# Moving 16 more tokens from the dense expert matmuls to the gathered rows, spreading the rows over the stages, and splitting pieces of u two ahead

## The chip, the cores and the metric

The kernel runs on one core of one Trainium2 chip. The metric is the device time of one execution in microseconds (us); less is better. Engines are named as in the profile: PE (TensorE matmul), PEld (TensorE weight load), DVE (VectorE), ACT (ScalarE), POOL (GpSimd) and SP (SyncE, which only issues DMAs here).

## The reference, cut to what matters

One layer over 512 tokens of width 2048. The change lies in its last part, a retrieval over 16384 experts of one neuron each: every token picks 16 experts in each of 8 heads (128 in all), and with the rows `u` and `v` of those experts

```
act = gelu(einsum('thkd,td->thk', u[ib], tb))
out = einsum('thk,thkd->td', g * act, v[ib])
```

Ahead of it stand an input projection, a state-space group, an attention group and an output projection; after it a norm.

## The kernel before, in words

Numbers are fp32. Each weight piece of 512 KB is loaded by SP (`w_raw`), copied by ACT to a rounded `w_hi` (L80) and completed by DVE with `w_lo = w_raw - w_hi` (L81, in `wload`); three matmuls (hi·hi, hi·lo, lo·hi) then make one product. There are 5 buffers for `w_raw` and 4 each for `w_hi` and `w_lo`.

The 512 tokens are treated in two ways. The first TD = 368 go through **dense** matmuls with all 16384 experts: `up` (L815, matmuls L823 to L825) multiplies 128 blocks of `u` with the tokens, `gate` (L897, L899) multiplies the result `A` by a matrix `G` that is zero where an expert was not picked, `down` (L927 to L929) multiplies by `v`. A group is 8 blocks; there are 16 groups, and a group has 384 matmuls in `up` and 384 in `down`, each with TD columns. The last 144 tokens are **gathered** (`gather`): POOL fetches, by an indirect DMA, for 128 tokens at a time one picked row of `u` or `v` each (L752, a tile of 128x2048 that the text calls a row tile), and DVE either dots it with the token (L757) or adds it, scaled, to the token's sum (L769). 128 tokens need 128 row tiles of `u` and 128 of `v`. The remaining X = 16 tokens are stacked so that one tile serves all of them with 128 / X = 8 picks each, which takes 16 tiles of `u` and 16 of `v`. So there are 288 row tiles.

The order in time: the trunk; the token routing's scores; a **routing stage**, in which `up` runs on PE for blocks of the first 10 groups while DVE and ACT do the routing (`topk`, then `gates`, which build `G` 4 tokens at a time: DVE L716 and L719, 4 small matmuls L729); `A` of these groups is parked in HBM (`Ad`). Then a **middle stage** with `up` and `down` of the last 6 groups, and a **late stage** in which POOL loads the parked `A` (L962) and only `down` runs.

`tick` sets the pace of the gather in program order: after each block of `up`, and twice per 512 columns of `down`, it adds a share of the row tiles that are left, divided by the ticks that are expected. A row tile's use on DVE stands two tiles behind its fetch (LAG = 2); the four buffers are `sx` tiles with the tag S:

```
self.owed += share * self.left / max(self.todo - 2, 1)
while self.owed >= 1 and self.left:
    self.owed -= 1
    self.left -= 1
    next(self.ga, None)
```

PE's order is that of the code from the routing stage's `up` on. The other engines' order is made by a scheduler when the program is built, and each engine's queue is in order on the chip.

Of the kernel before, what the change touches and what calls it, by code (L numbers as in the profile page):

```python
# [19 lines left out]
P = 128  # L20
# [3 lines left out]
KC = 16  # L24
# [5 lines left out]
NE = 16384  # L30
DT = 3
DN = DT * P
X = 16
XS = P // X
TD = DN - X
GB = 8
# [2 lines left out]
NTG = -(-TD // TG)  # L39
NEG = -3.0e38  # L40
LATE = 9
G_FIRST = 0.3
LAG = 2
SIDE0 = -8.0
SIDE = 0.65
# [13 lines left out]
class K:  # L59
# [724 lines left out]
    def peer_init(self):  # L784
        self.NG = P // GB
        self.turn_ = 0
        self.Gd = self.dp.tile([P, NTG, P, TG], F32, name="Gd")
        self.idxx = self.cp.tile([P, X], U32, name="idxx")
        self.gx = self.cp.tile([P, X], F32, name="gx")
        self.Ad = {}  # L790
        self.idx3 = self.cp.tile([P, P], U32, name="idx3")
        self.g3 = self.cp.tile([P, P], F32, name="g3")
        self.ga = None
        self.left = 2 * (P + X)
        self.todo = LATE * GB * G_FIRST + (self.NG - LATE) * GB + (self.NG - 1) * GB
        self.owed = 0.0

    def tick(self, share=1.0):
# [13 lines left out]
        tag = ("mm", "at", "mm", "tp")[self.turn_]  # L812
        return self.pp.tile([P, TD], F32, name=tag, tag=tag, bufs=4 if tag == "mm" else 2)

    def up(self, hi, engines, side=None):  # L815

        nc = self.nc
        Th, Tl = self.T2
        A = self.sx.tile([P, HB, TD], F32, name="A", tag="A", bufs=2)
        for i in range(HB):  # L820
            ps = self.bank() if side is None else self.pp.tile([P, TD], F32, name="mm", tag="mm", bufs=4)
            for kc, wh, wl in self.wpieces(self.io["uT"][hi * HB + i], KC, (8, P), engines):
                nc.tensor.matmul(ps, wh, Th[:, kc, :TD], start=(kc == 0), stop=False)  # L823
                nc.tensor.matmul(ps, wh, Tl[:, kc, :TD], start=False, stop=False)  # L824
                nc.tensor.matmul(ps, wl, Th[:, kc, :TD], start=False, stop=(kc == KC - 1))  # L825
                if side and kc % 4 == 3:
                    side()
            nc.scalar.activation(A[:, i, :], ps, AF.Gelu)
            self.tick(G_FIRST if side else 1.0)
        return A  # L830

    def peer_prologue(self, tk, top):

        nc = self.nc
        self.peer_init()

        def main():
            ready = None
            for t in (DT,) + tuple(reversed(range(DT))) + (None,):
                if t is not None:  # L840
                    res = {}
                    for d in self.topk(t, tk, top[0][t], top[1][t], res):
                        yield d, None
                    if t == DT:
                        nc.vector.tensor_copy(self.idx3, res["eu"])
                        nc.vector.tensor_copy(self.g3, res["g"])
                        self.ga = self.gather()
                        continue
                    if t == DT - 1:
                        for i in range(XS):  # L850
                            ps_, js = slice(i * X, (i + 1) * X), slice(i * X, (i + 1) * X)
                            nc.sync.dma_start(self.idxx[ps_, :], res["eu"][P - X:, js])
                            nc.sync.dma_start(self.gx[ps_, :], res["g"][P - X:, js])
                    steps = self.gates(t, tk, res)
                    for d in steps:
                        if d[0] is None:
                            break
                        yield d
                if ready:
                    yield from ready  # L860
                ready = steps

        m, state, later = main(), {"due": SIDE0, "on": True}, []

        def side():
            for w in later[:]:
                w[0] -= 1
                if w[0] <= 0:
                    later.remove(w)
                    w[1]()  # L870
            state["due"] += SIDE
            while state["due"] > 0:
                d = next(m, None)
                if d is None:
                    state["on"] = bool(later)
                    return
                state["due"] -= d[0]
                if d[1]:
                    later.append([12 if d[1].__name__ == "turn" else 3, d[1]])

        hi = 0
        with self.tc.manual_schedule(engines={nc.tensor.engine}):
            while state["on"] or hi % 2:
                A = self.up(hi, (nc.vector,), side)
                self.Ad[hi] = self.dp.tile([P, HB, TD], F32, name=f"Ad{hi}")
                nc.scalar.dma_start(self.Ad[hi], A)
                hi += 1
        return hi // 2
# [54 lines left out]
    def peer(self, es, first):  # L943
# [11 lines left out]
        for gi in list(range(first, self.NG)) + list(range(first)):  # L955
            As = []
            for hi in (2 * gi, 2 * gi + 1):
                if gi >= first:
                    A = self.up(hi, (nc.vector,))
                else:  # L960
                    A = self.sx.tile([P, HB, TD], F32, name="A", tag="A", bufs=2)
                    nc.gpsimd.dma_start(A, self.Ad[hi])  # L962
                self.gate(hi, A, fu)
                As.append(A)
            if before:
                self.down(*before)
            before = gi, self.split(As, fu)
            if gi == self.NG - 1:
                x1 = self.t2.tile([P, DT, D], F32, name="x1e", tag="T2h", bufs=1)
# [106 lines left out]
```

## Time and profile before

| what | value |
|---|---|
| median of three runs | 3438.3 us (3426.32 to 3446.59) |
| profiled execution | 3429.34 us, span 3426.5 us |
| PE busy | 3278.7 us, 96% |
| DVE busy | 2313.2 us, 68% |
| DMA | 770.10 MB, mean 225 GB/s |

The span is the time from the first to the last instruction; it is 2.84 us less than the execution's own time. The profiled execution lies 9 us under the median. A busy share is a mean over stages that differ much; it says nothing about which engine a stage waits for.

### The profile page before, as it was taken

What the parts mean: (1) busy time and instruction counts of PE and PEld (TensorE: products, weight loads), DVE (VectorE), ACT (ScalarE), POOL (GpSimd) and SP (SyncE); (2) the same over time, 40 slices, a digit from 0 to 9 for tenths busy, and PEclk for the clock granted to TensorE, in tenths of its full rate; (3) what the DMA queues carried; (4) which work ended last, traced back from release to release, by engine and by line L of the source; (5) the groups of instructions that cost most, each with busy time, mean ns of one, the idle gap of its engine ahead of it and who ended that gap; (6) DMA issues with size and microseconds to landing.
All of it is one profiled execution on the core that took longest, in us unless ns stands there. A gap on an engine that the chain in (4) does not pass through costs nothing.

```text
span 3426.5 us, 46085 instructions
## 1 busy us (share of the span) xinstructions
PE 3278.7 (96%) x18217; PEld 3032.9 (89%) x18217; DVE 2313.2 (68%) x3287; ACT 1195.4 (35%) x1956; POOL 866.7 (25%) x539
## 2 busy tenths in 40 slices
PE   6999999999899989999999999999999999989997
PEld 4777866678799989999999999999999999889987
DVE  6475345552435896466665888888878888788885
ACT  3342233332322323463666323323322322222222
POOL 2000000001111251012000443343445444544440
PEclk9999999999899999999999999999999999999999
DMA  3333322124322356466667998898998989899983
GB/s 134 98 102 99 111 74 68 63 95 138 121 90 87 105 197 224 161 227 223 220 229 254 342 362 328 335 353 325 357 371 324 352 324 344 311 340 320 342 321 118
DMA packets 207770, 770.10 MB, mean 225 GB/s; under 512 B 19441, under 2 KB 27633, under 8 KB 166449
## 3 DMA queue, kind: packets, MB, share of 16 engines
q1 hardware_dynamic: 146464, 375.06, 31.9%
q0 software_dynamic: 51408, 344.35, 26.5%
q10 hardware_dynamic: 9680, 47.75, 3.6%
q8 instruction: 142, 2.33, 0.3%
q14 instruction: 76, 0.61, 0.1%
HBM read 718.18 MB, written 48.89 MB: 224 GB/s over the span
## 4 chain that ended last, share of the span: by engine, by line
PE 69%; DMA 11%; DVE 9%; issue 6%; POOL 4%; ACT 1%; DVEq 0%; POOLq 0%; SPq 0%; ACTq 0%
PE mm L825 7%; PE mm L823 7%; PE mm L824 7%; DMA row<-in_v_dram,idx 5%; PE mm L116 3%; PE mm L118 3%; PE mm L117 3%; PE mm L102 3%; PE mm L104 3%; PE mm L103 3%; DVE w_lo L81 2%; DMA A<-Ad 2%; PE mm L927 2%; PE mm L928 2%; PE mm L929 2%
## 5 line engine op out<-in xcount | busy, mean ns | idle before, releaser
L80 ACT ACTIVATE w_hi<-w_raw 128x1024 fp32r<-128x1024 f32 x666 | 704.1, 1060 | 1667.6 <-PE mm L928 553.8
L81 DVE TENSOR_TENSOR w_lo<-w_raw,w_hi 128x1024 fp32r<-128x1024 f32 x648 | 811.7, 1263 | 610.8 <-ACT w_hi L80 599.6
L825 PE MATMUL mm<-T2h,w_lo 128*128 128x368 f32 x1664 | 549.6, 330 | 23.2 <-DVE w_lo L81 23.2
L823 PE MATMUL mm<-T2h,w_hi 128*128 128x368 f32 x1664 | 558.8, 336 | 0.5 <-ACT w_hi L80 0.5
L824 PE MATMUL mm<-T2l,w_hi 128*128 128x368 f32 x1664 | 547.3, 329 | 0.0
L752 POOL DMA_INDIRECT row<-in_u_dram,idx x128 | 197.5, 1543 | 788.2 <-DVE row L757 761.0
L769 DVE SCALAR_TENSOR_TENSOR x2g<-row,act,x2g 128x2048 f32<-128x2048 f32 x128 | 321.8, 2514 | 102.3 <-DMA row<-in_v_dram,idx 95.6
L928 PE MATMUL mm<-Wl,w_hi 128*128 128x368 f32 x1024 | 343.3, 335 | 0.0
L927 PE MATMUL mm<-Wh,w_hi 128*128 128x368 f32 x1024 | 343.0, 335 | 0.0
L929 PE MATMUL mm<-Wh,w_lo 128*128 128x368 f32 x1024 | 342.0, 334 | 0.0
L825 PEld LDWEIGHTS mm<-T2h,w_lo 128*128 128x128 f32 x1664 | 313.9, 189 | 29.3 <-DVE w_lo L81 29.3
L757 DVE SCALAR_TENSOR_TENSOR row<-row,h2n 128x2048 f32<-128x2048 f32 x128 | 323.3, 2543 | 0.0
L823 PEld LDWEIGHTS mm<-T2h,w_hi 128*128 128x128 f32 x1664 | 314.5, 189 | 1.0 <-ACT w_hi L80 0.9
L824 PEld LDWEIGHTS mm<-T2l,w_hi 128*128 128x128 f32 x1664 | 314.5, 189 | 0.0
L752 POOL DMA_INDIRECT row<-in_v_dram,idx x128 | 221.4, 1729 | 260.1 <-DVE x2g L769 227.3
L929 PE MATMUL at<-Wh,w_lo 128*128 128x368 f32 x512 | 175.3, 342 | 54.2 <-DVE w_lo L81 54.2
L116 PE MATMUL mm<-w_hi,T_hi 128*128 128x512 f32 x512 | 205.3, 401 | 0.0
L118 PE MATMUL mm<-w_hi,T_lo 128*128 128x512 f32 x512 | 203.3, 397 | 0.0
L117 PE MATMUL mm<-w_lo,T_hi 128*128 128x512 f32 x512 | 201.5, 394 | 0.0
L927 PEld LDWEIGHTS mm<-Wh,w_hi 128*128 128x128 f32 x1024 | 196.6, 192 | 0.0
L929 PEld LDWEIGHTS mm<-Wh,w_lo 128*128 128x128 f32 x1024 | 195.8, 191 | 0.0
L928 PEld LDWEIGHTS mm<-Wl,w_hi 128*128 128x128 f32 x1024 | 195.7, 191 | 0.0
(303 smaller groups left out, 6288.6 us busy)
## 6 DMA issues: line engine op xcount, KB each, us to landing
w_raw<-in_uT_dram SPq DMA_DIRECT2D x256, 512.0 KB
w_raw<-in_v_dram SPq DMA_DIRECT2D x256, 512.0 KB
w_raw<-in_wT_dram SPq DMA_DIRECT2D x58, 512.0 KB
Gd<-gb ACTq DMA_DIRECT2D x24, 1024.0 KB
G<-Gd POOLq DMA_DIRECT2D x32, 768.0 KB, 6.2
w_raw<-in_wN_dram SPq DMA_DIRECT2D x32, 512.0 KB
w_raw<-in_wo_dram SPq DMA_DIRECT2D x32, 512.0 KB
w_raw<-in_wq_dram SPq DMA_DIRECT2D x32, 512.0 KB
```

What stands on the lines that cost most here:

```text
L80: nc.scalar.activation(hi, raw, AF.Copy)
L81: sub = eng.tensor_sub(lo, raw, hi.bitcast(F32))
L116: nc.tensor.matmul(ps[t], Th[:, kc, s], wh, start=(kc == 0), stop=False)
L752: nc.gpsimd.indirect_dma_start(out=row, out_offset=None, in_=src, in_offset=bass.IndirectOffsetOnAxis(ap=idx[:, j:j + 1], axis=0))
L757: nc.vector.scalar_tensor_tensor(row, row, 1.0, h, op0=OP.mult, op1=OP.mult, accum_out=act[:, j:j + 1])
L769: nc.vector.scalar_tensor_tensor(acc, row, act[:, j:j + 1], acc, op0=OP.mult, op1=OP.add)
L823: nc.tensor.matmul(ps, wh, Th[:, kc, :TD], start=(kc == 0), stop=False)
L824: nc.tensor.matmul(ps, wh, Tl[:, kc, :TD], start=False, stop=False)
L825: nc.tensor.matmul(ps, wl, Th[:, kc, :TD], start=False, stop=(kc == KC - 1))
L927: nc.tensor.matmul(ps[j], vh, wh, start=f, stop=False)
L928: nc.tensor.matmul(ps[j], vh, wl, start=False, stop=False)
L929: nc.tensor.matmul(ps[j], vl, wh, start=False, stop=l)
```

## The change: what it does

X goes from 16 to 32. TD falls from 368 to 352, so all 12288 dense matmuls have 16 columns less. `NTG`, the number of 32-token pieces of the dense tokens, falls from 12 (the last one half full) to 11, so `gates` has 88 steps instead of 96, and the multiplication by `G` on POOL is one instruction instead of two. The stacked tokens take 32 + 32 row tiles instead of 16 + 16: 320 in all.

The pace: in the routing stage a block's tick counts 0.9 instead of 0.3, and in the late stage 0.9 instead of 1. `todo` follows. `upieces` replaces `wpieces` in `up`: in the routing stage it emits load and split of a piece of `u` two pieces before its matmuls, elsewhere just before them, as it was.

```diff
-X = 16
+X = 32
-G_FIRST = 0.3
+G_FIRST = 0.9
+G_LAST = 0.9
-        self.todo = LATE * GB * G_FIRST + (self.NG - LATE) * GB + (self.NG - 1) * GB
+        self.todo = LATE * GB * (G_FIRST + G_LAST) - GB * G_LAST + (self.NG - LATE) * GB * 2
-    def up(self, hi, engines, side=None):
+    def up(self, side=None):
-            for kc, wh, wl in self.wpieces(self.io["uT"][hi * HB + i], KC, (8, P), engines):
+            for kc, wh, wl in self.upieces(2 if side else 0):
+    def upieces(self, ahead):
+        for i in range(2):
+            while len(self.pre) <= ahead and self.npre < 2 * P:
+                b, k0 = self.npre // 2, 8 * (self.npre % 2)
+                self.pre.append(self.wload(self.io["uT"][b][:, k0:k0 + 8, :], [P, 8, P], self.nc.vector))
+                self.npre += 1
+            hi, lo = self.pre.pop(0)
+            for k in range(8):
+                yield 8 * i + k, hi[:, k, :], lo[:, k, :]
-                self.down(*before)
+                self.down(*before, 1.0 if gi >= first else G_LAST)
```

How it moves instructions, at three places.

POOL at the end of the routing stage, up to the first load of `G` (`tk_sel` belongs to `topk`, `row` is a row tile). Before:

```order
L752 DMA row<-in_u_dram,idx_8153 128x2048 x9
L673 TENSOR_TENSOR tk_sel<-tk_sel,tk_code 128x400 x11
L752 DMA row<-in_u_dram,idx_8153 128x2048
L673 TENSOR_TENSOR tk_sel<-tk_sel,tk_code 128x400
L752 DMA row<-in_u_dram,idx_8153 128x2048
L673 TENSOR_TENSOR tk_sel<-tk_sel,tk_code 128x400 x4
L752 DMA row<-in_u_dram,idx_8153 128x2048 x14
L894 DMA G<-Gd 128x12x128
```

The same place in the change:

```order
L753 DMA row<-in_u_dram,idx_8153 128x2048 x26
L674 TENSOR_TENSOR tk_sel<-tk_sel,tk_code 128x400
L753 DMA row<-in_u_dram,idx_8153 128x2048
L674 TENSOR_TENSOR tk_sel<-tk_sel,tk_code 128x400 x11
L753 DMA row<-in_u_dram,idx_8153 128x2048 x8
L674 TENSOR_TENSOR tk_sel<-tk_sel,tk_code 128x400 x4
L753 DMA row<-in_u_dram,idx_8153 128x2048 x37
L906 DMA G<-Gd 128x11x128
```

Counted over the whole queue, 32 row tiles stand ahead of the first load of `G` before and 84 in the change; between it and the first load of a parked `A` 133 and 134; from there on 123 and 102.

DVE in the routing stage, where one token tile's `topk` has ended and the next tile's routing steps have not come. Before:

```order
L666 CAST tk_pf<-tk_pu 128x128
L81 TENSOR_TENSOR w_lo<-w_raw,w_hi 128x1024 x4
L757 SCALAR_TENSOR_TENSOR row,act<-row,h2n 128x2048
L81 TENSOR_TENSOR w_lo<-w_raw,w_hi 128x1024 x6
L757 SCALAR_TENSOR_TENSOR row,act<-row,h2n 128x2048
L81 TENSOR_TENSOR w_lo<-w_raw,w_hi 128x1024 x4
```

In the change:

```order
L667 CAST tk_pf<-tk_pu 128x128
L82 TENSOR_TENSOR w_lo<-w_raw,w_hi 128x1024
L758 SCALAR_TENSOR_TENSOR row,act<-row,h2n 128x2048
L82 TENSOR_TENSOR w_lo<-w_raw,w_hi 128x1024 x2
L758 SCALAR_TENSOR_TENSOR row,act<-row,h2n 128x2048 x2
L82 TENSOR_TENSOR w_lo<-w_raw,w_hi 128x1024 x2
L758 SCALAR_TENSOR_TENSOR row,act<-row,h2n 128x2048
L82 TENSOR_TENSOR w_lo<-w_raw,w_hi 128x1024
L758 SCALAR_TENSOR_TENSOR row,act<-row,h2n 128x2048
L82 TENSOR_TENSOR w_lo<-w_raw,w_hi 128x1024
```

About every piece of `u` now has a dot of a row tile beside it. Counted per 10 pieces (`w_lo`) on DVE's queue, the routing stage has 1 to 3 uses of row tiles before, and 2 to 8 (mostly 6 to 8) in the change; the middle stage 7 or 8 in both; the late stage 7 or 8 before, and 6 or 7 in the change.

POOL in the late stage, one group of `down` (two loads of a parked `A`, two multiplications by `G`). Before:

```order
L962 DMA A<-Ad_10704 128x1472
L752 DMA row<-in_v_dram,idx_8153 128x2048
L897 TENSOR_TENSOR A<-A,G 128x4x352
L899 TENSOR_TENSOR A<-A,G 128x4x16
L752 DMA row<-in_v_dram,idx_8153 128x2048 x3
L894 DMA G<-Gd 128x12x128
L752 DMA row<-in_v_dram,idx_8153 128x2048 x8
L962 DMA A<-Ad_11117 128x1472
L752 DMA row<-in_v_dram,idx_8153 128x2048
L897 TENSOR_TENSOR A<-A,G 128x4x352
L899 TENSOR_TENSOR A<-A,G 128x4x16
L894 DMA G<-Gd 128x12x128
```

In the change:

```order
L974 DMA A<-Ad_10070 128x1408
L753 DMA row<-in_v_dram,idx_8153 128x2048
L909 TENSOR_TENSOR A<-A,G 128x1408
L753 DMA row<-in_v_dram,idx_8153 128x2048 x2
L906 DMA G<-Gd 128x11x128
L753 DMA row<-in_v_dram,idx_8153 128x2048 x7
L974 DMA A<-Ad_10418 128x1408
L753 DMA row<-in_v_dram,idx_8153 128x2048
L909 TENSOR_TENSOR A<-A,G 128x1408
L906 DMA G<-Gd 128x11x128
```

The shape of the group stays; it has about two row tiles less and one multiplication by `G` where there were two instructions.

## Rows read from the trace of the kernel before

**Rows 1.** The page: busy time of each engine, and the bytes moved in 40 equal slices of the span.

```profile
span 3426.5 us, 46085 instructions
...
PE 3278.7 (96%) x18217; PEld 3032.9 (89%) x18217; DVE 2313.2 (68%) x3287; ACT 1195.4 (35%) x1956; POOL 866.7 (25%) x539
...
GB/s 134 98 102 99 111 74 68 63 95 138 121 90 87 105 197 224 161 227 223 220 229 254 342 362 328 335 353 325 357 371 324 352 324 344 311 340 320 342 321 118
```

**Rows 2.** Busy time by stage: the stretch (us from the span's start), its length, busy time and count of instructions of each engine, granted clock of TensorE, busy share of the DMA engines, GB/s. The stages are the trunk with the scores, the routing stage, the middle stage, the late stage, the last `down`.

```profile
0.00:1127.00 1127.00, 1079.05 (x5063) 851.74 (x5063) 539.74 (x1165) 369.83 (x627) 83.01 (x60) 0.99 0.31 98
1127.00:1889.00 762.00, 738.31 (x4635) 731.65 (x4635) 519.43 (x1044) 380.83 (x834) 127.58 (x97) 0.99 0.58 206
1889.00:2595.00 706.00, 705.39 (x4210) 705.08 (x4209) 591.84 (x509) 220.55 (x249) 310.96 (x170) 1.00 0.92 348
2595.00:3338.00 743.00, 687.88 (x3922) 680.66 (x3921) 615.53 (x516) 205.00 (x214) 342.97 (x212) 0.96 0.89 330
3338.00:3426.50 88.50, 68.04 (x395) 63.74 (x394) 46.71 (x57) 19.17 (x34) 2.13 (x2) 0.92 0.34 127
```

**Rows 3.** The same view for single stretches of 100 us: one of the trunk, in which all matmuls have 512 columns; one early in the routing stage; two at the end of the middle stage.

```profile
800.00:900.00 100.00, 100.00 (x430) 80.43 (x429) 28.54 (x25) 23.24 (x33) 12.07 (x8) 1.00 0.30 95
1200.00:1300.00 100.00, 84.59 (x463) 81.08 (x462) 93.96 (x277) 28.75 (x35) 50.42 (x38) 0.95 0.56 195
...
2400.00:2500.00 100.00, 100.00 (x599) 100.00 (x598) 86.19 (x69) 31.04 (x34) 43.02 (x23) 1.00 0.95 359
2500.00:2600.00 100.00, 99.39 (x594) 99.08 (x593) 83.18 (x60) 31.20 (x34) 46.27 (x26) 1.00 0.97 363
```

**Rows 4.** Who waited for whom, PE alone: us in total, times, longest. First the routing stage, then the middle stage, then the late stage.

```profile
PE mm L825 <- DVE w_lo L81: 23.2, 19, 3.5
...
PE at L929 <- DVE w_lo L81: 0.6, 1, 0.6
...
PE at L929 <- DVE w_lo L81: 52.9, 21, 6.7
```

**Rows 5.** The same view for the late stage: DVE, then POOL.

```profile
DVE x2g L769 <- DMA row<-in_v_dram,idx: 95.6, 25, 6.4
...
POOL A L897 <- DMA A<-Ad: 125.9, 19, 10.5
```

**Rows 6.** Instructions of POOL in order of time, in the late stage, for one group: start, duration, instruction, and in brackets its idle time before it and what ended that.

```profile
3028.61 0.57 POOL L962 DMA_DIRECT2D A<-Ad  x1 [1.46 <-DVE Wl L909]
3030.84 0.96 POOL L752 DMA_INDIRECT row<-in_v_dram,idx  x1 [1.66 <-DVE x2g L769]
3037.85 4.95 POOL L897 TENSOR_TENSOR A<-A,G 128x1408 f32<-128x1408 f32 x1 [6.05 <-DMA A<-Ad]
3042.74 2.38 POOL L899 TENSOR_TENSOR A<-A,G 128x64 f32<-128x64 f32 x1
...
3046.53 0.57 POOL L962 DMA_DIRECT2D A<-Ad  x1
3047.41 1.96 POOL L752 DMA_INDIRECT row<-in_v_dram,idx  x1 [0.30 <-issue]
3057.75 3.23 POOL L897 TENSOR_TENSOR A<-A,G 128x1408 f32<-128x1408 f32 x1 [8.38 <-DMA A<-Ad]
...
3061.42 2.87 POOL L752 DMA_INDIRECT row<-in_v_dram,idx  x1 [0.16 <-issue]
```

**Rows 7.** Instructions of DVE in order of time, the same group.

```profile
3060.93 2.47 DVE L769 SCALAR_TENSOR_TENSOR x2g<-row,act,x2g 128x2048 f32<-128x2048 f32 x1 [6.14 <-DMA row<-in_v_dram,idx]
3063.33 2.35 DVE L81 TENSOR_TENSOR w_lo<-w_raw,w_hi 128x1024 fp32r<-128x1024 f32 x2
```

**Rows 8.** The routing stage, groups of instructions on DVE, then the small matmuls of `gates` on PE: shapes, count, busy us and mean ns of one, idle time before them and what ended it.

```profile
L81 DVE TENSOR_TENSOR w_lo<-w_raw,w_hi 128x1024 fp32r<-128x1024 f32 x160 | 199.3, 1254 | 146.4 <-ACT w_hi L80 146.3
L757 DVE SCALAR_TENSOR_TENSOR row<-row,h2n 128x2048 f32<-128x2048 f32 x30 | 70.6, 2354 | 0.0
L719 DVE TENSOR_TENSOR ga_A<-iota,ga_tr 128x512 f32<-128x512 f32 x96 | 66.9, 697 | 87.7 <-PE at L729 46.5 <-PE tp L729 41.1
L716 DVE TENSOR_TENSOR ga_B<-iota,ga_tr 128x512 f32<-128x512 f32 x96 | 65.7, 684 | 0.1
...
1652.52 1.05 PE L729 MATMUL tp<-ga_A,ga_B 128*128 128x128 f32 x8
1653.32 0.41 PE L823 MATMUL mm<-T2h,w_hi 128*128 128x368 f32 x1
```

**Rows 9.** DMA issues: count, KB each, median us to landing; and the second of the two multiplications by `G` in the late stage (count, busy us, mean ns).

```profile
G<-Gd POOLq DMA_DIRECT2D x32, 768.0 KB, 6.2
...
A<-Ad POOLq DMA_DIRECT2D x20, 736.0 KB, 9.7
...
L899 POOL TENSOR_TENSOR A<-A,G 128x64 f32<-128x64 f32 x20 | 25.7, 1284 | 0.0
```

More of the change, by code (lines that the diff above doesn't have):

```diff
@@ L879, in side @@
                     later.append([12 if d[1].__name__ == "turn" else 3, d[1]])
-        hi = 0
+        hi, self.pre, self.npre = 0, [], 0
         with self.tc.manual_schedule(engines={nc.tensor.engine}):
             while state["on"] or hi % 2:
-                A = self.up(hi, (nc.vector,), side)
+                A = self.up(side)
                 self.Ad[hi] = self.dp.tile([P, HB, TD], F32, name=f"Ad{hi}")
@@ L958, in peer @@
                 if gi >= first:
-                    A = self.up(hi, (nc.vector,))
+                    A = self.up()
                 else:
```

## The prediction

> **What bounds the kernel now.** I read the page first: PE is busy 96% of the span, DVE 68%, and the bytes moved rise from about 100 GB/s in the trunk to 310 to 371 in the second half [rows 1]. So a mean says little, and the next view is busy time by stage. The reader is to see four regimes in it [rows 2]. The trunk is untouched by the change. In the routing stage (762 us) PE is busy 738 us at 206 GB/s. In the middle stage (706 us) PE never rests and the DMA engines are busy 0.92 at 348 GB/s: here PE's matmuls alone set the time. In the late stage (743 us) PE is busy only 688 us, its granted clock is 0.96, and fewer bytes move, 330 GB/s. The waits say why. In the routing stage PE waits 23.2 us for `w_lo`, in the middle stage 0.6 us, in the late stage 52.9 us [rows 4]. Who holds `w_lo` up late? DVE waits 95.6 us for row tiles, and POOL, which issues them, stands 125.9 us waiting for parked `A` [rows 5]. In order of time it is one chain: POOL issues the load of `A` at 3028.61, waits, multiplies until 3045, issues the next load, waits 8.38 us, multiplies, and from 3030.84 to 3061.42 it has issued a single row tile, at 3047.41 [rows 6]. DVE runs out of row tiles, waits 6.14 us at 3060.93, and only then makes the next two `w_lo` [rows 7].
>
> How much does the late stage lose? In the middle stage, with PE always busy, 4210 matmuls take 706 us, 167.7 ns each [rows 2]. The late stage's 3922 would take 657.7 us at that pace; it takes 743, so 85 us are lost.
>
> **The matmuls' width.** A stretch in which all matmuls have 512 columns runs 430 in 100 us, 232.6 ns each [rows 3], against 167.7 ns at 368. That is 64.9 ns for 144 columns, 0.451 ns a column, so 16 columns are 7.2 ns. At 352 I take 160.5 ns. Where PE sets the time, 12288 matmuls give 88 us. The Trainium skill (TensorE: Matmul & The Clock Gate, Back-to-back issue gap) gives N/2.4 + 2.5 ns for a matmul at full clock; that is 155.8 ns at 368, where the trace has 167.7, and it would make the saving 6.67 ns and 82 us instead of 88. The measurement decides.
>
> **Routing stage.** 80 blocks of 48 matmuls save 3840 x 7.2 ns = 27.6 us. `gates` has 8 steps of 4 small matmuls less; 8 of these take 0.80 us until the next matmul starts [rows 8], so 32 are 3.2 us. Against that stand 52 more row tiles on DVE at 2354 ns (and about 0.08 us each to read the sum out, an estimate), 126 us, less 8 x (697 + 684) ns = 11 us of `gates` [rows 8]. DVE's 519 us become 634 of about 750, 85%; the middle stage has 592 of 706, 84%, and PE does not wait there [rows 2]. On the mean it fits. It doesn't fit everywhere: around 1200 to 1300 DVE is at 94% and PE falls to 84.6% [rows 3]; in this `topk` stretch the order has 4 row tiles more, 9.4 us. Where `gates` is dense, 10 pieces of `u` have some 28 instructions of it and 6.5 row tiles on DVE: 12 + 15.8 + 19.3 = 47 us, against 10 x 24 x 160.5 ns = 38.5 us of matmuls and 56 small ones at 0.1 us, 44 us in all. That is 3 us over for 10 pieces at worst, for some 35 of 160 pieces; with the idle ends between I take 10 us. Two pieces ahead (7.7 us of matmuls) can take back at most the 23.2 us that PE waits now [rows 4]; the added row tiles eat that cushion, and I take 0 for it. Sum: -27.6 - 3.2 + 9.4 + 10 = **-11 us**. Bounds: -54 (nothing added shows, the whole wait goes) and +120 (below).
>
> **Middle stage.** PE would need 4210 x 160.5 ns = 675.7 us, 30 us less. Row tiles are 134 against 133. The bytes stay: 348 GB/s x 706 us = 245.7 MB, plus one row tile (128 x 2048 x 4 bytes = 1.05 MB), less 12 loads of `G` smaller by a twelfth of 768 KB [rows 9], 245.9 MB. At PE's new pace that is 364 GB/s. No stretch shown holds that: two full-PE stretches run at 359 and 363 GB/s with the DMA engines 0.95 and 0.97 busy [rows 3]. Between the stage's mean of 348 and these I take 355: 693 us, **-13 us** (bounds 0 and -30).
>
> **Late stage.** PE's floor is 3922 x 160.5 ns = 629.5 us. The bytes are 330 x 743 = 245.2 MB less 21 row tiles (22.0), less 20 loads each of smaller `G` and `A` (1.3 and 0.7): 221.2 MB. At the rate of before, 330 GB/s, this takes 670 us; at the middle stage's 348, 636. What sets the rate is the chain, not the engines, which are only 0.89 busy [rows 2]. The chain is shorter by the second multiplication, 1.28 us for each `A` [rows 9], and DVE asks for a row tile every 629.5 / 102 = 6.2 us instead of 657.7 / 123 = 5.3 us, so the 30 us of [rows 6] starve it of five tiles instead of six. That favours the low end of the gain, and I take 335 GB/s: 660 us, **-83 us** (bounds -28, if the lost 85 us stay whole, and -113, if they vanish).
>
> **Last `down`.** 395 x 7.2 ns: **-3 us**. The pace's end fits better, too: 7 row tiles stand behind the last `A` instead of 13, which is in the late stage's sum.
>
> The stacked tokens' smaller edits (4 loads of `hx` instead of 8, routing indices in 4 loads instead of 8, on queues that do not hold PE) I cost at nothing; they hide under PE's matmuls. If they delayed DVE they would show in the routing stage, where the bound of +120 holds them.
>
> Sum: -11 - 13 - 83 - 3 = -110 us. Made against the profiled execution's 3429.3 us this is **3319 us**; that execution lies 9 us under the median, so a median of many runs would be some 9 us higher, well inside the range. About 0.5% (17 us) is what a measurement of this kernel can tell from no change; the runs of before spread over 20 us.
>
> **The rivals.**
>
> *The bytes flow as fast as asked for, up to a ceiling (20%).* If the late stage's chain is broken by the lower demand, PE or the DMA ceiling is left. With 361 GB/s, the mean of the two stretches of [rows 3], the middle stage takes 681 us (-25) and the late stage PE's 629.5 (-113): -11 - 25 - 113 - 3 = -152, **3277 us**. For it speaks that PE is full at 0.97 DMA share; against it that the late stage is not held by bandwidth. The Trainium skill (DMA: Bandwidth & Descriptors, Specifications) puts a core's share of HBM at about 358 GB/s; the trace's 363 is just over it, and with 358 the middle stage would be 687 us and the sum 3283.
>
> *The chain in the late stage stays as it is (15%).* The waits for parked `A`, 9.7 us from issue to landing [rows 9], and the order around them are unchanged. Then the 85 us stay: 629.5 + 85.3 = 715 us (-28), and if the middle stage can't exceed 348 GB/s it saves nothing. -11 + 0 - 28 - 3 = -42: **3387 us**.
>
> *Slower: DVE's queue sets the routing stage (6%).* DVE stands idle there some 248 us: 146.4 for `w_hi`, which waits for PE to free buffers, 87.7 for PE's small matmuls [rows 8], and a rest. If these waits are dictated by order and not by slack, the added work lies on top: 634 + 248 = 882 us instead of 762, +120 instead of -11, and **3450 us**, slower by 0.6%. It decides from the point where the stage takes 861 us, 99 more than before, which is what the other three stages give. Against it: both waits are waits for PE, so a later DVE finds them shorter. The remaining 4% are mixtures that end within 0.5%.
>
> **How the numbers follow.** Forecast 55%, the flowing bytes 20%, the unchanged chain 15%, slower 6%, near no change 4%. The first three end over 0.5% faster, so 0.90 faster, 0.04 same, 0.06 slower. The range takes the first three with some room: 3255 (below the ceiling case by the 23.2 us of the routing stage's waits) to 3395; the slow case lies outside.
>
> **What the profile would show.** Right: 100 us of the middle stage hold over 610 matmuls, with PE's wait near zero; the late stage is about 660 us long with 335 GB/s or more, PE's wait for `w_lo` there is roughly half of 53 us, DVE's wait for row tiles well under 96 us, and the granted clock is above 0.96. The routing stage moves about 280 GB/s with DVE near 85%, and is some 750 us long, PE's wait there no smaller than 23 us. Wrong: a routing stage longer than 800 us; PE waiting in the middle stage for `w_lo` whose cause is a DMA of `w_raw`, which would mean the rate of 348 was already the ceiling; or a late stage whose waits for `A` and row tiles add up as before.

## The result, and the profile after

The changed kernel takes 3319.9 us (median of four runs, 3313.6 to 3324.5) against 3437.7 us (3426.3 to 3446.6) for the kernel before, measured beside it: a ratio of 0.966 (95% interval 0.963 to 0.969). The forecast was 3319. The total is right, its terms are not: what the forecast gave to the routing stage has the wrong sign, and two others, for the middle and the late stage, were too small by about as much together.

The profiled execution took 3313.6 us. First its page, busy time of each engine.

```profile
span 3311.9 us, 45983 instructions
...
PE 3171.9 (96%) x18153; PEld 2926.7 (88%) x18153; DVE 2372.4 (72%) x3315; ACT 1175.1 (35%) x1908; POOL 882.6 (27%) x535
```

Then the changed kernel's routing, middle and late stage, in the columns of [rows 2].

```profile
1125.00:1904.00 779.00, 722.45 (x4590) 712.42 (x4589) 638.87 (x1141) 365.35 (x793) 231.16 (x155) 0.97 0.74 275
1904.00:2581.50 677.50, 676.91 (x4227) 676.62 (x4227) 583.91 (x445) 220.19 (x249) 282.71 (x155) 1.00 0.95 356
2581.50:3221.00 639.50, 622.07 (x3843) 618.60 (x3843) 560.99 (x502) 199.08 (x210) 285.18 (x165) 0.99 0.94 349
```

In the routing stage PE is now idle 56.5 us (779.0 - 722.45) where it was idle 24 [rows 2], and its granted clock has gone from 0.99 to 0.97. The middle stage is full of matmuls as before, only narrower: 677.5 us / 4227 = 160.3 ns each. In the late stage PE is idle 17 us where it was idle 55. In the routing stage the bytes have gone from 206 to 275 GB/s.

To compare kernels, all stages below are cut at the same events: the first matmul of the first group of `u` (start of the routing stage), that of the eleventh group (start of the middle stage), the first matmul of the sixth `down` (start of the late stage) and of the sixteenth, and the end of the span. By these marks, in us, from one profiled execution each:

| stage | before | after | difference | forecast |
|---|---|---|---|---|
| routing | 764.8 | 779.2 | +14.4 | -11 |
| middle | 708.6 | 677.3 | -31.3 | -13 |
| late | 729.6 | 639.2 | -90.4 | -83 |
| last `down` | 99.0 | 91.0 | -8.0 | -3 |
| span | 3426.5 | 3311.9 | -114.6 | -110 |

One stretch of 100 us of the middle stage answers to [rows 3], and then PE's waits to [rows 4]: three lines of the routing stage, one of the late stage.

```profile
2400.00:2500.00 100.00, 100.00 (x627) 100.00 (x626) 87.86 (x65) 32.11 (x35) 38.69 (x23) 1.00 0.91 341
```

```profile
PE mm L826 <- DVE w_lo L82: 33.3, 19, 6.4
PE tp L730 <- ACT ga_A L723: 19.1, 5, 8.6
PE at L730 <- ACT ga_A L723: 3.3, 3, 1.4
...
PE at L941 <- DVE w_lo L82: 15.5, 10, 4.0
```

The waits for `ga_A` (L730 are the small matmuls of `gates`) stand in no row of before: 22.4 us that are new. In the late stage PE's wait for `w_lo` fell from 52.9 to 15.5 us. The rows that answer to [rows 5], DVE and POOL in the late stage, say why:

```profile
DVE accx L770 <- DMA row<-in_v_dram,idxx: 18.2, 5, 6.9
DVE row L758 <- DMA row<-in_u_dram,idxx: 15.4, 6, 5.7
DVE x2g L770 <- DMA row<-in_v_dram,idx: 9.5, 6, 5.3
...
POOL A L909 <- DMA A<-Ad: 95.9, 19, 9.3
```

DVE's waits for row tiles fell from 106.3 us (the 95.6 of [rows 5] and 10.7 in two smaller lines) to 43.1 (these three), POOL's wait for parked `A` only from 125.9 to 95.9.

**Where the routing stage lost its time.** ACT's queue shows it. Its wait for the writes of `Gd` before the change:

```profile
ACT gb L731 <- DMA Gd<-gb: 56.0, 17, 6.7
```

and after it:

```profile
ACT gb L732 <- DMA Gd<-gb: 96.0, 18, 10.2
```

In `gates` the lines are these, unchanged but for their numbers (the scaling of `ga_A`, L723, stands ahead of `mm` in each step):

```
gb = [up.tile([P, 64, TG], F32, name="gb", tag="gb", bufs=2) for _ in range(2)]
...
        for i in range(2):
            nc.scalar.activation(gb[i][:, :, k4:k4 + 4], ...)
        if k4 + 4 == TG:
            for i in range(2):
                nc.scalar.dma_start(self.Gd[...], gb[i])
```

A piece is 32 tokens and fills two tiles; the tag has two buffers, and both belong to the same piece. So there is no second pair to fill while the first is on its way to HBM. One such place in the trace of the changed kernel, ACT in order of time:

```profile
1684.76 0.63 ACT L732 ACTIVATE gb<-at 128x256 f32<-128x256 f32 x2
1685.15 0.89 ACTq L736 DMA_DIRECT2D Gd<-gb  x2
1695.07 0.39 ACT L732 ACTIVATE gb<-tp 128x256 f32<-128x256 f32 x1 [9.68 <-DMA Gd<-gb]
1695.35 1.27 ACT L723 ACTIVATE ga_A<-ga_A,ga_tr 128x128 f32<-128x128 f32 x4
1696.52 0.45 ACT L829 ACTIVATE A<-mm 128x352 f32<-128x352 f32 x1
1700.16 0.38 ACT L732 ACTIVATE gb<-tp 128x256 f32<-128x256 f32 x1 [3.20 <-DMA Gd<-gb]
```

PE at the same place:

```profile
1693.68 0.32 PE L826 MATMUL mm<-T2h,w_lo 128*128 128x352 f32 x1
1695.79 1.68 PE L730 MATMUL tp<-ga_A,ga_B 128*128 128x128 f32 x8 [1.79 <-ACT ga_A L723]
1697.13 0.64 PE L824 MATMUL mm<-T2h,w_hi 128*128 128x352 f32 x1
```

And three short stretches, in the columns of [rows 2]:

```profile
1684.00:1694.00 10.00, 10.00 (x68) 9.71 (x66) 7.38 (x10) 1.39 (x3) 1.68 (x1) 1.00 1.00 374
1694.00:1697.00 3.00, 1.21 (x8) 1.21 (x8) 0.00 (x0) 1.89 (x6) 0.00 (x0) 0.92 1.01 423
1697.00:1700.00 3.00, 3.00 (x13) 3.00 (x12) 2.49 (x2) 0.00 (x0) 0.00 (x0) 0.51 0.42 172
```

ACT issues two writes of 1 MB (128 x 64 x 32 x 4 bytes) at 1685.15. The DMA engines are full (share 1.00, 374 GB/s). ACT's next instruction wants the first tile back and stands 9.68 us; for the second it stands until 1700.16. Behind it on ACT's queue is the scaling of `ga_A`; for that the small matmuls wait, and since PE's order is that of the code, the matmuls of `up` behind them wait too. PE stops for 1.79 us, and from 1697 to 1700 it is granted 0.51, the lower of its two levels (1.2 GHz), where it had 1.00 before the stop: 13 instructions in 3 us against 68 in 10.

### The profile page after: what moved, and what is told of

Read it like the earlier page. It is cut to its first block, busy times and chain, and to the rows that moved or that the text cites. A ratio compares the mean times of both kernels' runs of the same rounds, so it can differ in the third digit from the quotient of the medians.

```text
span 3311.9 us, 45983 instructions
## 1 busy us (share of the span) xinstructions
PE 3171.9 (96%) x18153; PEld 2926.7 (88%) x18153; DVE 2372.4 (72%) x3315; ACT 1175.1 (35%) x1908; POOL 882.6 (27%) x535
## 4 chain that ended last, share of the span: by engine, by line
PE 35%; DMA 7%; issue 5%; DVE 3%; POOL 2%; ACT 1%; DVEq 0%; POOLq 0%; ACTq 0%
PE mm L826 4%; PE mm L824 4%; PE mm L825 4%; PE mm L939 3%; PE mm L941 3%; PE mm L940 3%; DMA Gd<-gb 2%; PE at L941 2%; PE tp L941 1%; PE tp L939 1%; PE tp L940 1%; PE at L939 1%; PE at L940 1%; DMA A<-Ad 1%; DVE w_lo L82 1%
## 5 line engine op out<-in xcount | busy, mean ns | idle before, releaser
L826 PE MATMUL mm<-T2h,w_lo 128*128 128x352 f32 x1664 | 543.8, 327 | 33.4 <-DVE w_lo L82 33.3
L824 PE MATMUL mm<-T2h,w_hi 128*128 128x352 f32 x1664 | 549.0, 330 | 0.8 <-ACT w_hi L81 0.8
L825 PE MATMUL mm<-T2l,w_hi 128*128 128x352 f32 x1664 | 540.7, 325 | 0.0
L753 POOL DMA_INDIRECT row<-in_u_dram,idx x128 | 207.4, 1620 | 555.8 <-DVE row L758 529.2
L770 DVE SCALAR_TENSOR_TENSOR x2g<-row,act,x2g 128x2048 f32<-128x2048 f32 x128 | 336.4, 2628 | 15.6 <-DMA row<-in_v_dram,idx 9.5
L939 PE MATMUL mm<-Wh,w_hi 128*128 128x352 f32 x1024 | 331.4, 324 | 0.0
L941 PE MATMUL mm<-Wh,w_lo 128*128 128x352 f32 x1024 | 331.1, 323 | 0.0
L940 PE MATMUL mm<-Wl,w_hi 128*128 128x352 f32 x1024 | 329.8, 322 | 0.0
L758 DVE SCALAR_TENSOR_TENSOR row<-row,h2n 128x2048 f32<-128x2048 f32 x128 | 305.5, 2401 | 19.0 <-DMA row<-in_u_dram,idx 19.0
L103 PE MATMUL mm<-T_hi,w_hi 128*128 128x512 f32 x464 | 190.3, 411 | 0.0
```

Source lines behind the costliest of these rows:

```text
L753: nc.gpsimd.indirect_dma_start(out=row, out_offset=None, in_=src, in_offset=bass.IndirectOffsetOnAxis(ap=idx[:, j:j + 1], axis=0))
L758: nc.vector.scalar_tensor_tensor(row, row, 1.0, h, op0=OP.mult, op1=OP.mult, accum_out=act[:, j:j + 1])
L770: nc.vector.scalar_tensor_tensor(acc, row, act[:, j:j + 1], acc, op0=OP.mult, op1=OP.add)
L939: nc.tensor.matmul(ps[j], vh, wh, start=f, stop=False)
L940: nc.tensor.matmul(ps[j], vh, wl, start=False, stop=False)
L941: nc.tensor.matmul(ps[j], vl, wh, start=False, stop=l)
```

## The experiments

Stages by the marks above, in us; "row tiles" is how many the program places in the routing, middle and late stage. "Lost late" is the late stage less PE's floor there, 3841 matmuls at 160.3 ns (615.7 us), or at 167.7 ns (644.1 us) where X = 16.

| kernel | median | routing | middle | late | row tiles | lost late |
|---|---|---|---|---|---|---|
| before | 3437.7 | 764.8 | 708.6 | 729.6 | 32 / 133 / 123 | 86 |
| after | 3319.9 | 779.2 | 677.3 | 639.2 | 84 / 134 / 102 | 24 |
| e1_x16 | 3367.0 | 772.9 | 710.7 | 665.2 | 80 / 117 / 91 | 21 |
| e2_x32_alone | 3386.9 | 738.7 | 678.0 | 740.7 | 34 / 149 / 137 | 125 |
| e3_no_ahead | 3324.8 | 782.8 | 676.9 | 647.4 | 85 / 133 / 102 | 32 |
| e4_tg16 | 3301.1 | 741.5 | 677.5 | 663.2 | 84 / 134 / 102 | 48 |
| e5_ghalf | 3291.5 | 743.2 | 675.9 | 654.1 | 84 / 134 / 102 | 38 |
| e6_pace | 3268.1 | 751.9 | 676.6 | 624.4 | 101 / 134 / 85 | 9 |
| e7_x64 | 3312.9 | 714.3 | 680.5 | 707.2 | 99 / 177 / 108 | |
| e8_before_tg16 | 3417.8 | 759.2 | 707.7 | 717.6 | 31 / 134 / 123 | 74 |
| e9_pace2 | 3274.5 | 763.7 | 684.2 | 613.4 | 118 / 134 / 68 | -2 |
| e10_no_ahead | 3266.3 | 752.1 | 675.6 | 623.6 | 103 / 132 / 85 | 8 |
| e11_pace_only | 3318.7 | 806.0 | 673.8 | 626.3 | 101 / 134 / 85 | 11 |

The medians are of four runs each (ten for e8). The experiments ran in three sets (e1 to e4, e5 to e8, e9 to e11), each with the kernel before beside it: 3434.6, 3430.6 and 3434.8 us; each ratio is against the runs of before of its own set. The stages are those of one profiled execution each.

### The change in its parts

**e1: all of the change but the width.**

```diff
-X = 32
+X = 16
```

> The changed kernel with X back at 16: the new pace and the two pieces ahead alone, TD = 368. 288 row tiles, of which 80 stand in the routing stage, 117 in the middle stage and 91 in the late stage (before: 32, 133, 123). Theory (the pace frees the late stage, the width pays on PE): the late stage (from the sixth group of down to the last one) falls from 730 us to 655 to 680 although its matmuls are as wide as before; the middle stage stays near 709 us, since PE sets it; the routing stage grows from 765 us to 790 to 810, because row tiles compete there with the writes of Gd and with DVE. In all 3380 to 3410 us, 0.983 to 0.992 of before. Rival (the narrower matmuls do it all): the late stage stays above 710 us and the time at 3430 us or more.

Measured: 3367.0 us, a ratio of 0.979 (0.976 to 0.982), below the 3380 to 3410 that were expected. Its routing, middle and late stage:

```profile
1126.00:1898.70 772.70, 747.72 (x4654) 740.18 (x4653) 630.92 (x1138) 382.36 (x841) 210.54 (x146) 0.99 0.74 269
1898.70:2609.40 710.70, 710.70 (x4225) 710.70 (x4224) 564.74 (x452) 220.95 (x249) 268.75 (x155) 1.00 0.87 323
2609.40:3274.60 665.20, 653.57 (x3842) 652.34 (x3841) 553.71 (x478) 200.66 (x209) 282.50 (x177) 0.99 0.88 321
```

PE's and POOL's waits in the late stage:

```profile
PE at L941 <- DVE w_lo L82: 8.8, 3, 4.8
...
POOL A L909 <- DMA A<-Ad: 112.3, 19, 10.4
```

At the old width and with the new pace the late stage loses 21 us instead of 86. POOL waits 112.3 us for parked `A` there, 11% less than the 125.9 of before, and PE waits 8.8. The pace, not the width, frees the late stage. In the routing stage 48 more row tiles than before cost 8 us, where I had expected 25 to 45; e8 comes back to this.

**e2: the width alone,** with the pace of before and pieces of `u` split just ahead of their use.

```diff
-G_FIRST = 0.9
-G_LAST = 0.9
+G_FIRST = 0.3
+G_LAST = 1.0
...
-            for kc, wh, wl in self.upieces(2 if side else 0):
+            for kc, wh, wl in self.upieces(0):
```

> The changed kernel with the old pace (0.3 and 1.0) and no piece ahead: X = 32 alone. 320 row tiles, 34 in the routing stage, 149 in the middle stage, 137 in the late stage. Theory: the routing stage is 730 to 745 us (765 before, less 31 us of PE work); the middle stage is now held by bytes, 16 row tiles more, 680 to 700 us instead of 677; the late stage asks for 14 row tiles more than before in less time and keeps its chain: 700 to 735 us. In all 3340 to 3390 us. Rival (the late stage's gain comes from the narrower matmuls, not from the pace): the late stage is 660 us or less and the time 3310 us or less.

Measured: 3386.9 us, 0.986 (0.984 to 0.987). The same three stages:

```profile
1125.00:1863.50 738.50, 713.27 (x4589) 706.24 (x4588) 522.73 (x1034) 365.53 (x792) 135.27 (x102) 0.99 0.62 216
1863.50:2541.50 678.00, 676.84 (x4227) 675.98 (x4226) 618.20 (x516) 220.08 (x249) 330.96 (x171) 1.00 0.99 381
2541.50:3282.00 740.50, 649.43 (x3841) 638.44 (x3841) 629.91 (x533) 198.75 (x209) 339.31 (x199) 0.94 0.92 343
```

PE's wait in the late stage:

```profile
PE at L941 <- DVE w_lo L82: 87.0, 29, 10.8
```

Three things follow. In the routing stage the width saves 26 us (764.8 to 738.7), near the 31 of the forecast's first two terms. In the middle stage PE stays full while 381 GB/s flow, so the limit of 355 GB/s in the forecast was none; the stage was not held by bytes, though I had expected that here. In the late stage 14 more row tiles eat the whole floor gain and more: 740.7 us against 729.6 (700 to 735 expected), with 87 us of PE's waits.

With e1, e2 and e3 measured beside the same runs of before (3434.6), and the two pieces ahead counted as nothing, the parts add up: the width is worth 47.7 us at the old pace (3434.6 - 3386.9) and 42.2 at the new one (3367.0 - 3324.8); the pace 67.6 and 62.1. Of the 88 us that narrower matmuls give PE, about half arrive: at the old pace the late stage loses the rest, at the new one the routing stage.

**e3: without the two pieces ahead.**

```diff
-            for kc, wh, wl in self.upieces(2 if side else 0):
+            for kc, wh, wl in self.upieces(0):
```

> The changed kernel without the two pieces ahead: row tiles 85, 133, 102. Theory (as predicted, the cushion is worth little): the routing stage is 779 us within 10, the time within 10 us of the change. Rival (the cushion is what lets 52 more row tiles stand on DVE): the routing stage is longer by 20 us or more, with PE's wait for w_lo there above 50 us instead of 33.

Measured: 3324.8 us, 0.967 (0.965 to 0.969), the changed kernel's time. PE's two largest waits in the routing stage:

```profile
PE mm L826 <- DVE w_lo L82: 41.7, 27, 4.0
PE tp L730 <- ACT ga_A L723: 7.1, 5, 2.7
```

PE's wait for `w_lo` in the routing stage is 8 us more, its wait for `ga_A` 12 us less than in the changed kernel, and the stage is as long (782.8 and 779.2). By halves, as in the table under e4, it takes 381.3 and 401.5 us against 371.8 and 407.2. One execution of each does not tell whether that is more than scatter. e10 asks again on the best version, where those writes are out of the way.

### What holds the routing stage

**e4: a second pair of `gb`.** Pieces of 16 tokens halve a tile, so four fit where two were.

```diff
-TG = 32
+TG = 16
...
-            gb = [up.tile([P, 64, TG], F32, name="gb", tag="gb", bufs=2) for _ in range(2)]
+            gb = [up.tile([P, 64, TG], F32, name="gb", tag="gb", bufs=4) for _ in range(2)]
```

> The changed kernel with the tiles gb of gates for 16 tokens instead of 32 and four of them instead of two, in the same memory, so that one pair is filled while the other is written to Gd. G in HBM then lies in runs of 256 B instead of 512 B. Theory (the routing stage's second half is held by the writes of Gd, on which ACT waits 96 us): ACT's wait for Gd falls below 40 us, PE's wait for ga_A (22 us) nearly goes, and the routing stage falls from 779 us to 750 to 765. The middle and late stages may lose 0 to 30 us by the shorter runs of G. Rival (DVE's added row tiles hold the routing stage): it stays at 775 us or more though ACT's wait for Gd falls.

Measured: 3301.1 us, 0.960 (0.958 to 0.962). The routing stage:

```profile
1125.00:1866.00 741.00, 713.01 (x4588) 705.74 (x4587) 641.89 (x1142) 370.13 (x792) 243.23 (x155) 0.99 0.79 289
```

PE's wait in it, and ACT's largest for `gb`:

```profile
PE mm L826 <- DVE w_lo L82: 27.3, 18, 5.5
...
ACT gb L732 <- PE tp L730: 44.9, 27, 3.4
```

The routing stage falls from 779.2 to 741.5 us with the same row tiles and the same work of DVE (641.9 us, now 87% of the stage). ACT's wait for `Gd` is gone; what it now waits for at `gb` is PE. PE's waits for `ga_A` are gone, and the clock is back at 0.99. All of the gain lies where `Gd` is written. By groups of eight blocks of `u`, in us:

| kernel | first five groups | last five groups |
|---|---|---|
| before | 375.9 | 388.8 |
| after | 371.8 | 407.2 |
| e2_x32_alone | 364.8 | 374.0 |
| e4_tg16 | 371.8 | 369.9 |

The writes begin at 1445 us, in the fifth group. Beside e2, 50 more row tiles cost e4 7 us in the first half and nothing in the second. The edit halves the writes as well as doubling the pairs, and these two are not told apart here: a second pair of the full size was not run.

The late stage lost 24 us (639.2 to 663.2). One candidate: with TG = 16 the load of `G` has runs of 256 bytes instead of 512. e5 tests it.

**e8: the same on the kernel before.**

```diff
-TG = 32
+TG = 16
...
-            gb = [up.tile([P, 64, TG], F32, name="gb", tag="gb", bufs=2) for _ in range(2)]
+            gb = [up.tile([P, 64, TG], F32, name="gb", tag="gb", bufs=4) for _ in range(2)]
```

> The kernel before with gb for 16 tokens and four tiles, and G in runs of 256 B; nothing else. Theory (the writes of Gd hold the routing stage only when many row tiles compete with them): ACT's wait for Gd goes (56 us before), but the routing stage stays at 755 to 765 us, since PE hardly waits for it there; the late stage loses 5 to 30 us by the short runs; time 3430 to 3460. Rival (the writes of Gd always held that stage): the routing stage falls by 20 us or more.

Measured: 3417.8 us, 0.997 (0.995 to 0.999), where 3430 to 3460 was expected. The routing stage gains 6 us, not 38; its row:

```profile
1126.50:1885.70 759.20, 738.60 (x4623) 732.22 (x4622) 519.07 (x1040) 378.91 (x817) 133.62 (x99) 0.99 0.60 207
```

ACT stood 56 us on those writes before the change, too, but hardly any of it reached PE. That is why the trace of before shows no wait of PE for it.

More row tiles beside the writes are not the whole reason why they cost PE in the change. e1 has them too, at the old width. Its last five groups, then those of the changed kernel, and ACT's wait for `Gd` in each of the two stretches:

```profile
1502.10:1898.70 396.60, 392.07 (x2519) 390.52 (x2518) 313.67 (x361) 226.01 (x559) 95.03 (x65) 1.00 0.83 304
1497.00:1904.30 407.30, 378.34 (x2453) 375.45 (x2453) 316.43 (x358) 212.54 (x520) 106.49 (x70) 0.97 0.80 302
...
ACT gb L732 <- DMA Gd<-gb: 51.6, 14, 8.2
ACT gb L732 <- DMA Gd<-gb: 79.3, 14, 10.2
```

Both move bytes at the same rate (304 and 302 GB/s), but in e1 ACT waits 28 us less, PE is idle 4.5 us instead of 29, and its clock stays at 1.00. At the old width the row tiles make this half 8 us longer (396.6 against 388.8), at the new width 33 (407.2 against e2's 374.0). So it takes the row tiles and the narrower matmuls together. Why the same traffic costs more at the narrower width is not shown; that shorter matmuls cover less of ACT's wait is a candidate that no run tests.

The late stage gained 12 us, which I had not expected and do not explain.

**e11: more row tiles early, with the old `gb`.**

```diff
-G_FIRST = 0.9
-G_LAST = 0.9
+G_FIRST = 1.1
+G_LAST = 0.75
```

> The change with the pace 1.1 and 0.75 and nothing else (gb for 32 tokens, two tiles): row tiles 101, 134, 85. Theory (the waits for the writes of Gd grow with the row tiles beside them): late stage 618 to 630 as in the fastest kernel, but the routing stage 785 to 805 us and ACT's wait for Gd above 96 us; time 3295 to 3325, about as the change. Rival (gb is of no account once the pace is right): 3285 us or less.

Measured: 3318.7 us, 0.966 (0.963 to 0.968): no change against the changed kernel. The routing stage:

```profile
1123.60:1929.50 805.90, 731.52 (x4590) 720.61 (x4589) 675.73 (x1174) 365.41 (x792) 281.82 (x172) 0.96 0.76 288
```

PE's wait for `ga_A` in it, and ACT's for `Gd`:

```profile
PE tp L730 <- ACT ga_A L723: 33.0, 8, 9.1
...
ACT gb L732 <- DMA Gd<-gb: 87.6, 16, 10.2
```

The late stage gives 13 us and the routing stage takes 27. PE's wait for `ga_A` rose from 19.1 to 33.0 us, the clock is at 0.96; ACT's own wait did not rise (87.6 us against 96.0), which was a miss: how long ACT stands in all does not tell what PE loses; what counts is how much of it PE cannot cover.

### What holds the late stage

**e5: `G` loaded by halves of the tokens for a whole group,** on top of e4, after both loads of `A`. The runs have 512 bytes again, and POOL multiplies in four halves.

```diff
+        n = NTG // 2
+        for s in range(2):
+            G = fu.tile([P, n, GB, TG], F32, name="G", tag="G", bufs=1)
+            nc.gpsimd.dma_start(G, self.Gd[:, s * n:(s + 1) * n, gi * GB:(gi + 1) * GB, :])
+            for k, A in enumerate(As):
+                Av = A[:, :, s * n * TG:(s + 1) * n * TG].rearrange("p n (g t) -> p n g t", t=TG)
+                nc.gpsimd.tensor_mul(Av, Av, G[:, :, k * HB:(k + 1) * HB, :].rearrange("p g n t -> p n g t"))
```

> The run before (gb for 16 tokens, four tiles) with G loaded for half of the tokens and both halves of a group at once, so that its runs are 512 B again; a group has two loads of G and four half-size multiplications, after both A are there. Theory (the 24 us that the late stage lost against the change, 663 instead of 639, come from the short runs of G): the routing stage stays at 741 us, the late stage comes back to 635 to 650, the time is 3275 to 3295. Rival (they come from anything else in the shift of the rows): the late stage stays above 655 us.

Measured: 3291.5 us, 0.959 (0.956 to 0.962). The late stage takes 654.1 us, with PE waiting 24.6 us for `w_lo` (30.4 in e4). That lies between what the two theories expected. 9 of the 24 us are back; e8, with the short runs, did not lose late at all, and e3 shows some 8 us of scatter between kernels that should be alike here. What e4 lost late stays open.

**e6: fewer row tiles late,** on top of e5.

```diff
-G_FIRST = 0.9
-G_LAST = 0.9
+G_FIRST = 1.1
+G_LAST = 0.75
```

> The run before with the pace 1.1 in the routing stage and 0.75 in the late stage: row tiles 101, 134, 85 instead of 84, 134, 102. Theory (what the late stage loses beyond PE's floor of 615 us hangs on how many row tiles are asked of POOL and DVE there, and the routing stage with free writes of Gd has room): late stage 618 to 632 us, routing stage 741 to 752, time 3260 to 3280. Rival (the loss is the wait for parked A alone): the late stage moves by less than 5 us. Rival 2 (DVE is full in the routing stage): the routing stage grows by 20 us or more.

Measured: 3268.1 us, 0.952 (0.949 to 0.955). The late stage:

```profile
2553.00:3177.40 624.40, 622.00 (x3842) 620.99 (x3841) 511.14 (x490) 199.82 (x209) 251.54 (x169) 0.99 0.91 327
```

PE's waits in it (together 2.3 of the 2.4 us that it is idle), and POOL's two largest:

```profile
PE at L939 <- ACT w_hi L81: 1.8, 1, 1.8
PE at L941 <- DVE w_lo L82: 0.5, 1, 0.5
...
POOL A L911 <- DMA A<-Ad: 77.3, 20, 6.9
POOL A L911 <- DMA G<-Gd: 68.3, 10, 9.5
```

POOL stands 145.6 us, more than the 125.9 of before [rows 5], and PE waits 2.3 us instead of 52.9. So POOL's waits have no price of their own: they cost PE only as far as DVE is asked for more row tiles than POOL can issue between them. With 68 asked for nothing is lost; with 85, 8 to 11 us; with 102, 24 to 48; with 123, 74 and 86; with 137, 125. e1 fits with 91 tiles and 21 us. The routing stage, freed of the `Gd` writes, takes 17 more tiles for 9 us, where e11 paid 27.

**e10: e6 without the two pieces ahead.**

```diff
-            for kc, wh, wl in self.upieces(2 if side else 0):
+            for kc, wh, wl in self.upieces(0):
```

> The fastest kernel so far without the two pieces ahead: row tiles 103, 132, 85. Theory (the cushion is worth little, as in the change, where its removal cost 5 us in the median): time within 12 us of 3268, routing stage 748 to 765. Rival (with more row tiles on DVE the cushion counts): the routing stage is longer by 20 us or more.

Measured: 3266.3 us, 0.951 (0.949 to 0.954), with the same stages as e6 within 1 us each. Splitting two pieces ahead is worth nothing, with the `Gd` writes in the way (e3) or without.

**e9: fewer still,** on top of e6.

```diff
-G_FIRST = 1.1
-G_LAST = 0.75
+G_FIRST = 1.3
+G_LAST = 0.6
```

> The fastest kernel so far (gb for 16 tokens, G by halves, pace 1.1 and 0.75) with the pace 1.3 and 0.6: row tiles 118, 134, 68. Theory (the late stage has nothing left to give, 624 us against PE's floor of 615, and 17 row tiles added on DVE cost the routing stage about 9 us, as the last 17 did): late stage 617 to 624, routing stage 758 to 775, time 3268 to 3285, no gain or a small loss. Rival (there is more to have from the late stage): 3260 us or less.

Measured: 3274.5 us, 0.953 (0.951 to 0.956): 8 us more than e10 in the same set, which four runs of each barely tell apart. The late stage stands at PE's floor, and the routing stage pays; these two stages:

```profile
1124.00:1887.80 763.80, 722.58 (x4591) 713.64 (x4590) 715.23 (x1212) 369.56 (x793) 316.90 (x191) 0.98 0.84 329
...
2572.00:3185.40 613.40, 611.09 (x3842) 610.52 (x3841) 482.10 (x473) 200.47 (x211) 218.42 (x151) 1.00 0.87 303
```

DVE is busy 94% of the routing stage, which is 12 us longer than in e6; the middle stage is 8 us longer (that it inherits a backlog is not shown). The best pace is near that of e6.

**e7: twice the width again,** X = 64, on top of TG = 16 and four `gb`, with `G` of a whole group loaded at once.

```diff
-X = 32
+X = 64
...
-        G = fu.tile([P, NTG, HB, TG], F32, name="G", tag="G", bufs=1)
-        nc.gpsimd.dma_start(G, self.Gd[:, :, hi * HB:(hi + 1) * HB, :])
+        if hi % 2 == 0:
+            self.Gp = fu.tile([P, NTG, GB, TG], F32, name="G", tag="G", bufs=1)
+            nc.gpsimd.dma_start(self.Gp, self.Gd[:, :, hi * HB:(hi + 2) * HB, :])
+        G = self.Gp[:, :, (hi % 2) * HB:(hi % 2 + 1) * HB, :]
```

> gb for 16 tokens as in the two runs before, X = 64: TD = 320, 384 row tiles (99, 177, 108). PE's work falls by another 88 us, the bytes rise by 67 MB. Theory (the middle stage is where the bytes become the limit; X = 32 alone ran it at 381 GB/s with the DMA engines 0.99 busy and PE just full): it needs about 290 MB, 760 us at 381 GB/s, where PE would need 646; late stage 600 to 670 us, routing stage 715 to 745; time 3310 to 3430, slower than with X = 32. Rival (PE's width is still what counts): 3240 us or less.

Measured: 3312.9 us, 0.966 (0.963 to 0.968). The middle and the late stage:

```profile
1836.80:2517.20 680.40, 640.67 (x4225) 633.51 (x4225) 626.98 (x458) 213.30 (x245) 320.38 (x173) 0.97 0.99 385
2517.20:3224.40 707.20, 613.36 (x3842) 602.60 (x3841) 603.91 (x553) 199.04 (x212) 286.21 (x171) 0.92 0.92 347
```

PE's wait in the late stage:

```profile
PE at L943 <- DVE w_lo L82: 88.7, 35, 8.3
```

That is slower than with X = 32 (e4 0.960, e5 0.959), as expected. In the middle stage PE is no longer what sets the time: the DMA engines are full at 385 GB/s, and PE is idle 40 us. ACT waits there 228 us for pieces of `w_raw`. That the bytes alone bound it is not shown, since DVE is 92% busy too (627 of 680 us). The stage was expected at 760 us and took 680, in part because it did not do all its work: of the 177 row tiles that the program places there 152 were issued in it. Some 10 of the others had already gone out in the routing stage, and some 15 fell to the late stage, which lost PE 88.7 us. Narrower matmuls pay as long as the row tiles that they cost find room.

## Why the prediction was right, and where it was wrong

**The width.** Right: 160.3 ns a matmul at 352 columns, forecast 160.5. The Trainium skill (TensorE: Matmul & The Clock Gate, Back-to-back issue gap) would have 149.2 by its N/2.4 + 2.5, which it gives for a single matmul by itself and not for a stream with weight loads; the trace does not agree, and the spacing read from the trace was the safer base.

**Middle stage, -13 forecast, -31.3 measured.** The step that failed is the choice of 355 GB/s as what the stage can move. The changed kernel needs 356 GB/s and PE is full; e2 moves 381 GB/s with PE full and e7 385 at a DMA share of 0.99. The stage can move at least 381, and 385 is the most that any run's stage shows, both above the two stretches of [rows 3], where the engines were only 0.95 and 0.97 busy because PE asked for no more. The stage came out at the rival's floor (681 us forecast there, 677.3 measured). The Trainium skill's 358 GB/s (DMA: Bandwidth & Descriptors, Specifications) would have erred the same way: no run here stops at it.

**Late stage with the last `down`, -86 forecast, -98.4 measured.** The mechanism was right: POOL's waits for parked `A` starve DVE of row tiles, and a lower demand takes away most of it. The mis-sized term is the loss that stays: 30 us forecast (660 - 629.5), 24 measured, from 86. The forecast counted the shorter multiplication and the narrower matmuls in its favour; e1 shows that the pace does it without them, and e2 that they do not do it without the pace. The rival in which the 85 us stay is refuted.

**Routing stage, -11 forecast, +14.4 measured.** Here the reasoning failed, and the table under e4 says in which half. The first two terms (-27.6 and -3.2) hold: e2 measures -26. Half of the -27.6 and the +9.4 for the `topk` stretch make -4.4 for the first five groups; measured -4.1. The step that failed is the +10 for dense `gates`: with the other half of the width and the -3.2 it makes -7 for the last five groups, and +18.4 was measured, as if the term had been 35. It looked for the price on DVE, where there is none: e4 carries the changed kernel's work of DVE there in 4 us less than e2 takes with less of it. What the forecast has no term for is a wait on ACT that was in the trace of before, where PE did not show it: 56 us for the writes of `Gd`. With the added row tiles beside those writes and the narrower matmuls (e1: with the row tiles alone it is 64 us), ACT stands 96 us, its stall reaches PE through `ga_A` (22.4 us; what it adds by way of `w_hi` and `w_lo` is not told apart), and PE loses 32 us of waiting and, with the clock going from 0.99 to 0.97, some 15 more (an estimate, 2% of 779 us), against 31 us of narrower matmuls. e4 takes 38 us of it away, e11 makes it worse; the rival with DVE's queue, the only slower one, is refuted by e4, where DVE is busier and the stage shorter. That rival's idle time of DVE, 248 us, is 243 by [rows 2] (762.0 - 519.4); the slip of 5 us changes no chance.

**Two pieces ahead, 0 forecast:** right (e3, e10).

**The sum.** The three errors are +25, -18 and -12 us, and -5 remains. That the total was met to 1 us is luck (from one profiled execution to the other, as the forecast was made, it was missed by 5); the middle and late terms were good to some 20 us.

**What the profile was to show.** 627 matmuls in 100 us of the middle stage (over 610 forecast) without waits: right. The late stage at 349 GB/s with a clock of 0.99 and DVE's waits at 43 us: right; PE's wait fell further than to half, and the stage is 639.5 us long, not about 660. The routing stage moves 275 GB/s (280 forecast) with DVE at 82% (85%), but takes 779 us instead of 750.

The best versions of these runs are e6 and the same without the pieces ahead (e10), which are not told apart: 0.952 and 0.951 of the kernel before, where the change alone has 0.966.

## What to carry to other kernels

When a change puts more traffic beside a stage, look at the waits for transfers on every in-order queue of that stage, also those that the bottleneck engine does not feel yet: a wait that is hidden by slack can get a price from the traffic that the change adds and from the slack that it takes away. Count double buffers in pieces, not in tiles: two buffers that both belong to one piece leave none to fill while they are written out. And where a mean rate is to be taken as a ceiling, see first whether anything asked for more.

## What the runs showed of the hardware that was not expected

One core moved 381 and 385 GB/s over 678 and 680 us (e2, e7) at a DMA share of 0.99, where 371 in one slice of the page was the most before. A stop of PE of 1.79 us was followed by a granted clock of 0.51 in the next 3 us, in which matmuls started every 0.29 us instead of 0.16: nine of them took 2.78 us where they would have taken some 1.5 at the faster spacing (an estimate), so the slow clock added 1.3 us or more to the stop.
